# Banded softmax attention in one launch: key low parts and values padded with zeros to 128 rows and 128 columns

## Chip, cores and metric

The kernel runs on one core of a Trainium2 chip. The metric is the device time of one execution in microseconds (us); the lower, the better.

## What is computed

The program is a network of two parts: a first block (a gated delta rule mixer and a convolutional gated feed-forward network) and then two equal layers. The change lies in one of the three mixers of each of these two layers, attention inside a band of 128 positions with a learned bias and a sink. Of 8 query heads, four each share one of two key and value heads (`kv`); a head has 64 features, the sequence 512 positions.

```python
def _window_gqa(q, k, v, rel_bias, sink):
    ...
    kb, vb = band(k), band(v)            # each block of 128 queries sees three blocks of keys
    ...
    s = jnp.einsum('bnqkgd,bnskd->bnkgqs', q, kb).astype(jnp.float32) * (C_DH ** -0.5) + bias
    s = jnp.where(valid[None, :, None, None], s, MASK_VALUE)
    sink_l = sink.astype(jnp.float32).reshape(C_KV_HEADS, G)[:, :, None, None]
    m = jnp.maximum(jnp.max(s, axis=-1, keepdims=True), sink_l)
    p = jnp.exp(s - m)
    p = p / (jnp.sum(p, axis=-1, keepdims=True) + jnp.exp(sink_l - m))
    o = jnp.einsum('bnkgqs,bnskd->bnqkgd', p.astype(v.dtype), vb)
    return o.reshape(Bsz, S, C_HEADS * C_DH)
```

Its result `y_c` goes through a projection, is gated, and is added to those of the two other mixers (`branch` c, a and b in the kernel).

## The kernel before, in words

Activations lie with features on the 128 partitions and the 512 positions along the free dimension. Weights come in tiles of 128 x 1024 by DMA, and each is split into a high part (fp32r, on ScalarE, line 110) and a low part (the rest, on VectorE or GpSimd, line 119). A projection is three products for each tile of 128 x 128 weights and 512 positions: lines 157 (high by high), 158 (high by low) and 159 (low by high). These three lines, "the GEMM products" below, are most of what TensorE does in the whole program.

`window` (lines 883 to 951; stage `win` in names of tiles) does one layer's banded attention. It first makes the keys. For each of the two key heads the 64 feature rows are copied to both halves of a tile `K`, 128 rows, as high parts; one shared tile `Kl` holds the low parts, head 0 in rows 0 to 63, head 1 in rows 64 to 127. Values are transposed into one tile `V`, for each block of 128 keys 64 columns of head 0 and 64 of head 1. Then come four strips `s`; a strip is one projection of two query heads, `h = s` with key head 0 and `h = s + 4` with key head 1. For one head:

- `qq` holds the query's high parts in the rows of its own key head (`R`, 64 rows) and its low parts in the other 64 rows.
- For each of four blocks of 128 queries, line 925 is the score product with `kh` over all 128 rows (high by high and low by high at once), and line 926 adds the high query parts by the low keys: 64 rows of `qq` and of `kl` alone. A block sees 256 or 384 keys.
- Lines 929 to 941 are the softmax on VectorE and ScalarE: bias, row maximum, exponential with its sum, sink, reciprocal, scaling.
- Line 944 transposes the 128 x 128 blocks of probabilities on TensorE, line 946 copies them out of PSUM, and line 948 is the value product: 64 columns of `V` (those of `kv`) give 64 rows `O[R]` of the output. The operands are plain f32, for which the trace shows two weight loads and two matmuls for each product.

After both heads of a strip the 128 x 512 output `O` is copied (line 950) and sent to DRAM (`keep_y`), from where branch c loads it.

Nothing writes out the order of the engines' queues by hand: a scheduler that goes by its own estimates of time lays the instructions of all stages into each engine's queue. In this stage it puts GEMM products of branch a (stage `br`) between the pieces of the window, so TensorE's queue holds window products and GEMM products in turn. An engine takes its queue in that order. The two layers have the same pattern of products in this stage.

In a row of the trace, `128*128` ahead of an operand's shape is the shape of TensorE's array that the instruction uses, rows by columns: 64*128 is half of the rows, 128*64 half of the columns.

Of the kernel before, what the change touches and what calls it, by code (L numbers as in the profile page):

```python
# [9 lines left out]
F32R = mybir.dt.float32r  # L10
# [7 lines left out]
P = 128  # L18
# [5 lines left out]
def f32(ap):  # L24
    return ap.bitcast(F32)
# [590 lines left out]
def window_bias_head(p, h):  # L616

    t = p.t("wb", 3, 384)
    dr = p.relrow[h]
    p.nc.sync.dma_start(t, bass.AP(dr.tensor, dr.offset + 127, [[511, 128], [1, 384]]))  # L620
    return t
# [94 lines left out]
def strip_r(p, name, b, tag="z", bufs=3, pool=None):  # L716

    ps = p.strip(name, b, p.X)
    t = p.t(tag, bufs, keep=tag[0] == "z", pool=pool)
    p.nc.vector.tensor_tensor(t, ps, p.r, MULT)  # L720
    return t
# [9 lines left out]
def keep_y(p, y, ys):  # L731
    d = p.dram([P, 512], "yd")
    p.nc.sync.dma_start(d, y)
    ys.append(d)


def side_by_side(p, ps, out, scale=None):

    nc = p.nc
    v = out.rearrange("p (h k c) -> p h k c", k=2, c=64)  # L740
    hi, lo = v[:, :, 0, :], v[:, :, 1, :]
    src = ps.rearrange("p (h c) -> p h c", c=64)
    if scale is None:
        nc.scalar.activation(hi, src, AF.Copy)
        nc.vector.tensor_tensor(lo, src, f32(hi), SUB)
    else:
        nc.scalar.activation(hi, src, AF.Identity, scale=scale)
        nc.vector.scalar_tensor_tensor(lo, src, scale, f32(hi), MULT, SUB)
    return out
# [4 lines left out]
def mla(p, l, G, low, mid, high):  # L754
# [45 lines left out]
    wvh, wvl = p.wload(f"w_uv{l}", 0, 1024)  # L800
    V = []
    for t in range(4):
        ps = p.ps()
        ts = slice(t * P, t * P + P)
        for k in range(2):
# [4 lines left out]
            nc.tensor.matmul(ps, xl[:, ts], wvh[:, c], start=False, stop=k == 1)  # L810
        V.append(side_by_side(p, ps, p.t("V", 4, 1024, F32R)))

# [14 lines left out]
    for pr in range(4):  # L827
# [6 lines left out]
        for hh in range(2):  # L834
# [10 lines left out]
            Q.append((qh, ql))  # L845
        Y = p.t("x", 3, keep=True)
        for hh in range(2):
            qh, ql = Q[hh]
            for q2 in range(2):
# [21 lines left out]
                for kb in range(4):  # L871
                    v = V[kb][:, (pr * 2 + hh) * P:(pr * 2 + hh) * P + P]
                    nc.tensor.matmul(o, v, pth[:, kb, :], start=kb == 0, stop=False)
                    nc.tensor.matmul(o, v, ptl[:, kb, :], start=False, stop=kb == 3)
                y = Y[half[hh], q2 * 256:q2 * 256 + 256]
                nc.scalar.copy(y, o[64:])
                nc.vector.tensor_tensor(y, o[:64], y, ADD)
        keep_y(p, Y, G.y["a"])

# [3 lines left out]
def window(p, l, G):  # L883
    nc = p.nc
    at = G.at
    w_in = f"w_in{l}"
    half = [slice(0, 64), slice(64, 128)]

    k = strip_r(p, w_in, at["ck"])
    K = []  # L890
    kl = p.t("Kl", 1, dtype=F32R)
    for kv in range(2):
        kh = p.t("K", 2, dtype=F32R)
        for i in range(2):
            nc.scalar.activation(kh[half[i]], k[half[kv]], AF.Copy)
        nc.vector.tensor_tensor(kl[half[kv]], k[half[kv]], f32(kh[half[kv]]), SUB)
        K.append((kh, kl))
    v = strip_r(p, w_in, at["cv"])
    pv = p.ps("b")
    for t in range(4):  # L900
        nc.tensor.transpose(pv[:, t * P:t * P + P], v[:, t * P:t * P + P], p.ident)
    V = p.t("V", 1)
    nc.scalar.copy(V, pv)
    for s in range(4):
        q = strip_r(p, w_in, at["cq2"] + s)
        O = p.ps("o")
        Y = p.t("x", 3, keep=True)
        for kv in range(2):
            h = s + 4 * kv
            R = slice(kv * 64, kv * 64 + 64)  # L910
            qq = p.t("Q", 8, dtype=F32R)
            nc.scalar.activation(qq[R], q[R], AF.Copy)
            nc.gpsimd.tensor_tensor(qq[half[1 - kv]], q[R], f32(qq[R]), SUB)
            kh, kl = K[kv]
            sink = p.col(f"sink{l}")[:, h:h + 1]
            wb = window_bias_head(p, h)
            negm, den, es = (p.small([P, 4], n, 3) for n in ("w4m", "w4d", "w4e"))
            E = []
            for qb in range(4):
                k0, k1 = max(qb - 1, 0), min(qb + 2, 4)  # L920
                W = (k1 - k0) * P
                qs = slice(qb * P, qb * P + P)
                ks = slice(k0 * P, k1 * P)
                sc = p.ps("a")[:, :W]
                nc.tensor.matmul(sc, qq[:, qs], kh[:, ks], start=True, stop=False)
                nc.tensor.matmul(sc, qq[R, qs], kl[R, ks], start=False, stop=True)
                sb = p.t("wsb", 10, 384)[:, :W]
                off = (k0 - qb + 1) * P
                nc.vector.tensor_tensor_reduce(sb, sc, wb[:, off:off + W], 0.125, sink, ADD, MAX,
                                               accum_out=negm[:, qb:qb + 1])  # L930
                nc.vector.tensor_scalar(negm[:, qb:qb + 1], negm[:, qb:qb + 1], -1.0, None, MULT)
                nc.scalar.activation(sb, sb, AF.Exp, bias=negm[:, qb:qb + 1], accum_out=den[:, qb:qb + 1])
                E.append(sb)
            nc.scalar.activation(es, negm, AF.Exp, bias=sink)
            nc.vector.tensor_tensor(den, den, es, ADD)
            nc.vector.reciprocal(den, den)
            for qb in range(4):
                k0, k1 = max(qb - 1, 0), min(qb + 2, 4)
                W = (k1 - k0) * P
                qs = slice(qb * P, qb * P + P)  # L940
                nc.vector.tensor_scalar(E[qb], E[qb], den[:, qb:qb + 1], None, MULT)
                pt = p.ps("b")[:, :W]
                for kb in range(k1 - k0):
                    nc.tensor.transpose(pt[:, kb * P:kb * P + P], E[qb][:, kb * P:kb * P + P], p.ident)
                pts = p.t("pts", 4, 384)[:, :W]
                nc.scalar.copy(pts, pt)
                for kb in range(k0, k1):
                    nc.tensor.matmul(O[R, qs], V[:, kb * P + kv * 64:kb * P + kv * 64 + 64],
                                     pts[:, (kb - k0) * P:(kb - k0) * P + P], start=kb == k0, stop=kb == k1 - 1)
        nc.scalar.copy(Y, O)  # L950
        keep_y(p, Y, G.y["c"])

# [15 lines left out]
def hgrn(p, l, G, pools, tail):  # L968
# [6 lines left out]
    p.rows_gemm(f"w_bi{l}", 0, p.X, pst)  # L975
    V = []
    for t in range(4):
# [170 lines left out]
def branch(p, l, G, pool, n):  # L1148

    nc = p.nc  # L1150
    bi = "abc".index(n)
    Y = [p.split(p.load(d, "yl", 2, pool=pool), "ys", 8, le="g", pool=pool) for d in G.y[n]]
    M = []
# [84 lines left out]
def layer(p, l):  # L1238
# [11 lines left out]
    with p.pool(f"br{l}") as br, p.pool(f"acc{l}") as G.pool:  # L1250
        p.stage = f"br{l}"
        p.WLO_SEQ = "g"
        branch(p, l, G, br, "b")
        p.WLO_SEQ = "v"
        with p.pool(f"win{l}"):
            p.stage = f"win{l}"
            window(p, l, G)
        with p.pool(f"M{l}"):
            p.stage = f"br{l}"
            for n in "ac":  # L1260
                M = branch(p, l, G, br, n)
            p.stage = f"wo{l}"
            out_proj(p, f"w_out{l}", M, p.col(f"g_x{l}"))
# [846 lines left out]
```

## Time and profile before

| | us |
|---|---|
| time, median of 3 runs | 3699.72 |
| the 3 runs | 3694.47 to 3702.97 |
| the profiled execution, its own time | 3706.06 |
| its span, first to last instruction | 3704.2 |
| TensorE busy in the span | 3523.1 (95%) |
| VectorE, ScalarE, GpSimd busy | 2342.8 (63%), 1715.5 (46%), 1190.2 (32%) |
| first score product to last value product, layer 0 | 1688.01 to 1823.66: 135.65 |
| the same, layer 1 | 2959.76 to 3095.41: 135.65 |

"TensorE busy" is the union of the matmuls' spans. These are longer than the distance between their starts, since matmuls overlap; a busy TensorE may still start its products late. The pace of a stretch is therefore read from the starts of its rows in the timeline, not from the busy share.

### The profile page before, as it was taken

Reading aid. Unit: us, or ns where it says so; the run is one execution under the profiler, and the core shown is the slowest. Engines: PE = TensorE matmul, PEld = TensorE weight load, DVE = VectorE, ACT = ScalarE, POOL = GpSimd, SP = SyncE. Lnnn points to the kernel's source line nnn. Section 1 sums busy time; section 2 is a strip of 40 time slices with the busy share of each in tenths; the row PEclk is TensorE's granted clock in tenths of the full one; section 3 lists DMA queues with packets and bytes.
Section 4 is the critical chain, followed back from the end, with each engine's and each line's share of the span. In section 5 each row is a group of like instructions: output and inputs, shape, how many; then the busy total and the mean of one; then the engine's idle time right before and its main releaser. Section 6 shows DMA issues by size and latency. Waiting matters only on the chain.

```text
span 3704.2 us, 51835 instructions
## 1 busy us (share of the span) xinstructions
PE 3523.1 (95%) x19504; PEld 2864.9 (77%) x19504; DVE 2342.8 (63%) x3681; ACT 1715.5 (46%) x3095; POOL 1190.2 (32%) x1109
## 2 busy tenths in 40 slices
PE   7998899989999999899999999998978999999998
PEld 6887788868888787687777888877767877778886
DVE  8878774755543777775556665358768655656643
ACT  3776554344433444565544444244436555444431
POOL 4475774422211333331121221124433312212212
PEclk9999898999999999899999999999989999999999
DMA  4345775533334222222253333421212322432332
GB/s 172 105 109 167 212 235 143 166 123 97 97 108 126 67 71 62 66 87 85 83 159 100 117 97 100 128 86 54 69 46 74 98 74 88 164 109 97 98 102 91
DMA packets 228955, 401.05 MB, mean 108 GB/s; under 512 B 77281, under 2 KB 118497, under 8 KB 228705
## 3 DMA queue, kind: packets, MB, share of 16 engines
q1 hardware_dynamic: 228704, 397.74, 35.0%
q8 instruction: 154, 2.52, 0.3%
q14 instruction: 97, 0.79, 0.1%
HBM read 347.58 MB, written 47.97 MB: 107 GB/s over the span
## 4 chain that ended last, share of the span: by engine, by line
PE 75%; DVE 13%; POOL 3%; issue 3%; ACT 3%; DMA 2%; SPq 0%; DVEq 0%; ACTq 0%; POOLq 0%
PE ffn_psg L158 4%; PE ffn_psg L159 4%; PE ffn_psg L157 4%; PE br_psg L159 4%; PE br_psg L158 3%; PE br_psg L157 3%; PE f_psg L159 2%; PE f_psg L158 2%; PE f_psg L157 2%; PE glu_psg L158 2%; PE glu_psg L159 2%; PE glu_psg L157 2%; PE hg_psg L159 2%; PE hg_psg L157 1%; PE hg_psg L158 1%
## 5 line engine op out<-in xcount | busy, mean ns | idle before, releaser
L159 PE MATMUL ffn_psg<-xo_X,ffn_wl 128*128 128x512 f32 x704 | 274.7, 390 | 0.0
L158 PE MATMUL ffn_psg<-xo_X,ffn_wh 128*128 128x512 f32 x704 | 273.9, 389 | 0.0
L157 PE MATMUL ffn_psg<-xo_X,ffn_wh 128*128 128x512 f32 x704 | 273.9, 389 | 0.0
L119 DVE TENSOR_TENSOR ffn_wl<-ffn_wr,ffn_wh 128x1024 fp32r<-128x1024 f32 x88 | 153.5, 1745 | 19.7 <-ACT ffn_wh L110 19.7
L157 PEld LDWEIGHTS ffn_psg<-xo_X,ffn_wh 128*128 128x128 f32 x704 | 132.1, 188 | 28.1 <-issue 0.5
L159 PEld LDWEIGHTS ffn_psg<-xo_X,ffn_wl 128*128 128x128 f32 x704 | 132.1, 188 | 27.6 <-issue 0.5
L158 PEld LDWEIGHTS ffn_psg<-xo_X,ffn_wh 128*128 128x128 f32 x704 | 132.1, 188 | 27.5
L720 DVE TENSOR_TENSOR ffn_z<-ffn_psg,xo_ry 128x512 f32<-128x512 f32 x88 | 60.7, 692 | 142.8 <-PE ffn_psg L159 142.6
L1232 POOL TENSOR_TENSOR ffn_z<-ffn_z,ffn_z 128x512 f32<-128x512 f32 x44 | 57.3, 1302 | 274.4 <-DVE ffn_z L720 233.8
L159 PE MATMUL f_psg<-ffn_U,f_wl 128*128 128x512 f32 x352 | 140.8, 400 | 0.0
L158 PE MATMUL glu_psg<-gout_X,glu_wh 128*128 128x512 f32 x352 | 137.9, 392 | 3.0 <-DVE gout_X L1368 3.0
L157 PE MATMUL glu_psg<-gout_X,glu_wh 128*128 128x512 f32 x352 | 138.1, 393 | 2.1 <-ACT gout_X L1367 2.1
L119 DVE TENSOR_TENSOR f_wl<-f_wr,f_wh 128x1024 fp32r<-128x1024 f32 (+1 forms) x48 | 56.8, 1183 | 129.6 <-ACT f_wh L110 129.6
L158 PE MATMUL f_psg<-ffn_U,f_wh 128*128 128x512 f32 x352 | 138.7, 394 | 0.0
L157 PE MATMUL f_psg<-ffn_U,f_wh 128*128 128x512 f32 x352 | 138.0, 392 | 0.0
L159 PE MATMUL glu_psg<-gout_X,glu_wl 128*128 128x512 f32 x352 | 137.6, 391 | 0.0
L1164 POOL TENSOR_TENSOR br_acc<-br_acc,br_za 128x512 f32<-128x512 f32 x32 | 44.7, 1398 | 285.7 <-DVE br_za L1163 233.7
L110 ACT ACTIVATE ffn_wh<-ffn_wr 128x1024 fp32r<-128x1024 f32 x88 | 93.7, 1064 | 92.1 <-PE ffn_psg L158 67.5
L110 ACT ACTIVATE f_wh<-f_wr 128x1024 fp32r<-128x1024 f32 (+1 forms) x48 | 47.5, 989 | 167.3 <-PE f_psg L158 134.7
L119 DVE TENSOR_TENSOR glu_wl<-glu_wr,glu_wh 128x1024 fp32r<-128x1024 f32 x44 | 56.4, 1282 | 102.0 <-ACT glu_wh L110 101.8
L110 ACT ACTIVATE br_wh<-br_wr 128x1024 fp32r<-128x1024 f32 x96 | 81.0, 844 | 83.4 <-PE br_psg L158 59.3
L110 ACT ACTIVATE hg_wh<-hg_wr 128x1024 fp32r<-128x1024 f32 x64 | 67.6, 1056 | 108.0 <-PE hg_psg L158 78.3
(853 smaller groups left out, 11558.2 us busy)
## 6 DMA issues: line engine op xcount, KB each, us to landing
ffn_wr<-in_f_w_dram SPq DMA_DIRECT2D x88, 512.0 KB, 3.5
hg_wr<-in_w_in_dram SPq DMA_DIRECT2D x56, 512.0 KB, 3.6
br_wr<-in_w_in_dram SPq DMA_DIRECT2D x48, 512.0 KB, 3.6
glu_wr<-in_ffn_in_dram SPq DMA_DIRECT2D x44, 512.0 KB, 3.5
fill_C<-in_w_mod_dram SPq DMA_DIRECT2D x64, 256.0 KB, 5.4
f_wr<-in_f_w_dram SPq DMA_DIRECT2D x32, 512.0 KB, 3.6
prep_wr<-in_gdn_in_dram SPq DMA_DIRECT2D x24, 512.0 KB, 3.7
fill_wr<-in_x_wk_dram SPq DMA_DIRECT2D x16, 512.0 KB, 4.5
```

Of the source, the lines that this page charges most:

```text
L110: nc.scalar.activation(hi, src, AF.Copy)
L119: e.tensor_tensor(lo, src, f32(hi), ALU.subtract)
L157: nc.tensor.matmul(ps, wh, xh, start=start, stop=False)
L158: nc.tensor.matmul(ps, wh, xl, start=False, stop=False)
L159: nc.tensor.matmul(ps, wl, xh, start=False, stop=stop)
L720: p.nc.vector.tensor_tensor(t, ps, p.r, MULT)
L1164: nc.gpsimd.tensor_tensor(G.acc[m], G.acc[m], a, ADD)
L1232: nc.gpsimd.tensor_tensor(z1, z1, z3, MULT)
```

## The change

- Each key head gets a `Kl` tile of its own, 128 rows, of which the 64 rows of the other head are set to zero on GpSimd. The second score product takes all 128 rows of `qq` and of `kl`. The rows added multiply low query parts by zero.
- Each key head gets a `V` tile of its own, with zeros in the 64 columns of the other head. The one copy out of PSUM becomes two strided copies of 64 columns a block, with one GpSimd memset each.
- A value product takes 128 columns and gives all 128 rows of `O`. The products of both heads add into the same region of PSUM, so one accumulation for each query block holds the key blocks of both heads, and is issued once the second head's probabilities are there (`T` keeps those of the first). `pts` has 8 buffers for that, where it had 4.

The number of score products, transposes and value products is the same as before.

```diff
--- before.py
+++ after.py
@@ -886,25 +886,33 @@
     w_in = f"w_in{l}"
     half = [slice(0, 64), slice(64, 128)]
 
+
     k = strip_r(p, w_in, at["ck"])
     K = []
-    kl = p.t("Kl", 1, dtype=F32R)
     for kv in range(2):
-        kh = p.t("K", 2, dtype=F32R)
+        kh, kl = p.t("K", 2, dtype=F32R), p.t("Kl", 2, dtype=F32R)
         for i in range(2):
             nc.scalar.activation(kh[half[i]], k[half[kv]], AF.Copy)
         nc.vector.tensor_tensor(kl[half[kv]], k[half[kv]], f32(kh[half[kv]]), SUB)
+        nc.gpsimd.memset(f32(kl[half[1 - kv]]), 0.0)
         K.append((kh, kl))
     v = strip_r(p, w_in, at["cv"])
     pv = p.ps("b")
     for t in range(4):
         nc.tensor.transpose(pv[:, t * P:t * P + P], v[:, t * P:t * P + P], p.ident)
-    V = p.t("V", 1)
-    nc.scalar.copy(V, pv)
+
+    V = []
+    for kv in range(2):
+        t = p.t("V", 2)
+        c = lambda a, i: a.rearrange("p (t i c) -> p t i c", t=4, i=2)[:, :, i]
+        nc.scalar.copy(c(t, kv), c(pv, kv))
+        nc.gpsimd.memset(c(t, 1 - kv), 0.0)
+        V.append(t)
     for s in range(4):
         q = strip_r(p, w_in, at["cq2"] + s)
         O = p.ps("o")
         Y = p.t("x", 3, keep=True)
+        T = {}
         for kv in range(2):
             h = s + 4 * kv
             R = slice(kv * 64, kv * 64 + 64)
@@ -923,7 +931,7 @@
                 ks = slice(k0 * P, k1 * P)
                 sc = p.ps("a")[:, :W]
                 nc.tensor.matmul(sc, qq[:, qs], kh[:, ks], start=True, stop=False)
-                nc.tensor.matmul(sc, qq[R, qs], kl[R, ks], start=False, stop=True)
+                nc.tensor.matmul(sc, qq[:, qs], kl[:, ks], start=False, stop=True)
                 sb = p.t("wsb", 10, 384)[:, :W]
                 off = (k0 - qb + 1) * P
                 nc.vector.tensor_tensor_reduce(sb, sc, wb[:, off:off + W], 0.125, sink, ADD, MAX,
@@ -942,11 +950,15 @@
                 pt = p.ps("b")[:, :W]
                 for kb in range(k1 - k0):
                     nc.tensor.transpose(pt[:, kb * P:kb * P + P], E[qb][:, kb * P:kb * P + P], p.ident)
-                pts = p.t("pts", 4, 384)[:, :W]
+                pts = p.t("pts", 8, 384)[:, :W]
                 nc.scalar.copy(pts, pt)
-                for kb in range(k0, k1):
-                    nc.tensor.matmul(O[R, qs], V[:, kb * P + kv * 64:kb * P + kv * 64 + 64],
-                                     pts[:, (kb - k0) * P:(kb - k0) * P + P], start=kb == k0, stop=kb == k1 - 1)
+                T[kv, qb] = pts
+                if kv == 1:
+                    for i in range(2):
+                        for kb in range(k0, k1):
+                            nc.tensor.matmul(O[:, qs], V[i][:, kb * P:kb * P + P],
+                                             T[i, qb][:, (kb - k0) * P:(kb - k0) * P + P],
+                                             start=i == 0 and kb == k0, stop=i == 1 and kb == k1 - 1)
         nc.scalar.copy(Y, O)
         keep_y(p, Y, G.y["c"])
 
```

On TensorE, layer 0, the first value products of strip 0, before (`pts` are the transposed probabilities, `psb` the transposes, `psa` the scores, `psg` a GEMM product):

```order
L157 MATMUL br0_psg_3570_17062<-br0_ys_3559_17013,br0_wh_3572_17065 128x512
L948 MATMUL win0_pso_3357_16276<-win0_pts_3373_16321,win0_V_3351_16241 64x128 x2
L948 MATMUL win0_pso_3357_16276<-win0_pts_3375_16330,win0_V_3351_16241 64x128 x3
L944 MATMUL win0_psb_3376_16336<-cstt_69,win0_wsb_3369_16303 128x128 x3
L944 MATMUL win0_psb_3378_16346<-cstt_69,win0_wsb_3371_16310 128x128 x2
L925 MATMUL win0_psa_3414_16474<-win0_K_3343_16195,win0_Q_3409_16466 128x256
L926 MATMUL win0_psa_3414_16474<-win0_Kl_3342_16194,win0_Q_3409_16466 128x256
L925 MATMUL win0_psa_3416_16481<-win0_K_3343_16195,win0_Q_3409_16466 128x384
L926 MATMUL win0_psa_3416_16481<-win0_Kl_3342_16194,win0_Q_3409_16466 128x384
L158 MATMUL br0_psg_3570_17062<-br0_ys_3560_17014,br0_wh_3572_17065 128x512
```

There a head's value products come ahead of its own later transposes. The same place on TensorE in the changed kernel, whose lines 933, 934, 952 and 959 are the old 925, 926, 944 and 948:

```order
L157 MATMUL br0_psg_3572_17069<-br0_ys_3561_17020,br0_wh_3574_17072 128x512
L952 MATMUL win0_psb_3378_16338<-cstt_69,win0_wsb_3371_16310 128x128 x3
L952 MATMUL win0_psb_3380_16345<-cstt_69,win0_wsb_3373_16317 128x128 x2
L959 MATMUL win0_pso_3359_16283<-win0_pts_3375_16328,win0_V_3352_16244 128x128 x2
L158 MATMUL br0_psg_3572_17069<-br0_ys_3562_17021,br0_wh_3574_17072 128x512
L159 MATMUL br0_psg_3572_17069<-br0_ys_3561_17020,br0_wl_3575_17073 128x512
L157 MATMUL br0_psg_3572_17069<-br0_ys_3564_17026,br0_wh_3574_17072 128x512
L158 MATMUL br0_psg_3572_17069<-br0_ys_3565_17027,br0_wh_3574_17072 128x512
L933 MATMUL win0_psa_3416_16481<-win0_K_3342_16194,win0_Q_3411_16473 128x256
L934 MATMUL win0_psa_3416_16481<-win0_Kl_3343_16195,win0_Q_3411_16473 128x256
L933 MATMUL win0_psa_3418_16488<-win0_K_3342_16194,win0_Q_3411_16473 128x384
L934 MATMUL win0_psa_3418_16488<-win0_Kl_3343_16195,win0_Q_3411_16473 128x384
```

The transposes and the scores of the next head stand where they stood, and of the value products only those of the first block are left here. The others have moved to where the second head's transposes are done; on TensorE, further on in strip 0 of the changed kernel:

```order
L933 MATMUL win0_psa_3437_16546<-win0_K_3344_16200,win0_Q_3432_16538 128x256
L934 MATMUL win0_psa_3437_16546<-win0_Kl_3345_16201,win0_Q_3432_16538 128x256
L959 MATMUL win0_pso_3359_16283<-win0_pts_3396_16393,win0_V_3353_16247 128x128 x2
L959 MATMUL win0_pso_3359_16283<-win0_pts_3377_16335,win0_V_3352_16244 128x128 x3
L959 MATMUL win0_pso_3359_16283<-win0_pts_3398_16404,win0_V_3353_16247 128x128 x3
L952 MATMUL win0_psb_3399_16413<-cstt_69,win0_wsb_3392_16375 128x128 x3
L959 MATMUL win0_pso_3359_16283<-win0_pts_3379_16342,win0_V_3352_16244 128x128 x3
L952 MATMUL win0_psb_3401_16426<-cstt_69,win0_wsb_3394_16382 128x128 x2
L933 MATMUL win0_psa_3439_16553<-win0_K_3344_16200,win0_Q_3432_16538 128x384
L934 MATMUL win0_psa_3439_16553<-win0_Kl_3345_16201,win0_Q_3432_16538 128x384
```

Value products of both heads (`V_3352` and `V_3353`) now alternate on the same output `pso_3359`.

On GpSimd, layer 0, ahead of the window, in the changed kernel (`br_wl` are low parts of the weights of branch b, `br_ys` inputs of branch a, line 921 is the old 913):

```order
L119 TENSOR_TENSOR br_wl_16081<-br_wr_16078,br_wh_16080 128x512
L897 MEMSET win_Kl_16195 64x512
L909 MEMSET win_V_16244 128x4x64
L119 TENSOR_TENSOR br_wl_16102<-br_wr_16099,br_wh_16101 128x1024
L119 TENSOR_TENSOR br_wl_16141<-br_wr_16138,br_wh_16140 128x512
L119 TENSOR_TENSOR br_ys_17009<-br_yl_17006,br_ys_17008 128x512
L119 TENSOR_TENSOR br_ys_17015<-br_yl_17012,br_ys_17014 128x512
L119 TENSOR_TENSOR br_ys_17021<-br_yl_17018,br_ys_17020 128x512
L119 TENSOR_TENSOR br_ys_17027<-br_yl_17024,br_ys_17026 128x512
L897 MEMSET win_Kl_16201 64x512
L909 MEMSET win_V_16247 128x4x64
L921 TENSOR_TENSOR win_Q_16285<-win_z_16281,win_Q_16285 64x512
```

The four memsets of a layer are the only rows that are new in this queue; the others stand in the order of before.

## Rows read from the trace of the kernel before

**Rows 1.** The page: busy time of the engines, share of the span, instructions

```profile
PE 3523.1 (95%) x19504; PEld 2864.9 (77%) x19504; DVE 2342.8 (63%) x3681; ACT 1715.5 (46%) x3095; POOL 1190.2 (32%) x1109
```

**Rows 2.** By stretch: us, busy PE PEld DVE ACT POOL, PEclk, DMA, GB/s

```profile
1840.00:1860.00 20.00, 20.00 (x88) 16.16 (x87) 13.09 (x18) 10.73 (x16) 2.93 (x3) 1.00 0.27 91
1688.01:1823.66 135.65, 135.65 (x656) 100.33 (x655) 69.80 (x197) 69.43 (x158) 24.62 (x17) 1.00 0.25 76
2959.76:3095.41 135.65, 135.65 (x656) 100.33 (x654) 69.79 (x197) 69.45 (x158) 24.63 (x17) 1.00 0.26 76
```

**Rows 3.** TensorE's groups in layer 0's window: count, busy us, mean ns, idle before

```profile
L948 PE MATMUL win_pso<-win_pts,win_V 128*64 128x128 f32 x160 | 22.2, 279 | 0.0
...
L926 PE MATMUL win_psa<-win_Kl,win_Q 64*128 64x384 f32 x16 | 7.0, 438 | 0.0
...
L926 PE MATMUL win_psa<-win_Kl,win_Q 64*128 64x256 f32 x16 | 6.1, 381 | 0.0
```

**Rows 4.** Timeline of TensorE, scores of two blocks: start us, us, line, shapes

```profile
1707.06 0.34 PE L925 MATMUL win_psa<-win_K,win_Q 128*128 128x384 f32 x1
1707.33 0.44 PE L926 MATMUL win_psa<-win_Kl,win_Q 64*128 64x384 f32 x1
1707.69 0.38 PE L925 MATMUL win_psa<-win_K,win_Q 128*128 128x256 f32 x1
1708.01 0.38 PE L926 MATMUL win_psa<-win_Kl,win_Q 64*128 64x256 f32 x1
1708.32 0.50 PE L159 MATMUL br_psg<-gl_X,br_wl 128*128 128x512 f32 x1
1708.66 0.40 PE L157 MATMUL br_psg<-br_ys,br_wh 128*128 128x512 f32 x1
```

**Rows 5.** The same view: value products ahead of transposes, then ahead of GEMM products

```profile
1717.77 0.39 PE L158 MATMUL br_psg<-gl_X,br_wh 128*128 128x512 f32 x1
1718.09 1.31 PE L948 MATMUL win_pso<-win_pts,win_V 128*64 128x128 f32 x10
1719.32 0.77 PE L944 MATMUL win_psb<-cstt,win_wsb 128*128 128x128 f32 x5
1719.84 0.42 PE L925 MATMUL win_psa<-win_K,win_Q 128*128 128x384 f32 x1
1720.19 0.43 PE L926 MATMUL win_psa<-win_Kl,win_Q 64*128 64x384 f32 x1
...
1730.24 0.40 PE L158 MATMUL br_psg<-gl_X,br_wh 128*128 128x512 f32 x1
1730.57 0.87 PE L948 MATMUL win_pso<-win_pts,win_V 128*64 128x128 f32 x6
...
1731.70 0.40 PE L157 MATMUL br_psg<-gl_X,br_wh 128*128 128x512 f32 x1
```

**Rows 6.** The same view: products of other stages that all use 128*128

```profile
1223.52 1.05 PE L1092 MATMUL hg_psa<-hg_hl,hg_ha 128*128 128x128 f32 x8
...
1954.04 0.28 PE L158 MATMUL cr_psa<-cr_K,cr_Q 128*128 128x256 f32 x1
...
1954.52 0.28 PE L157 MATMUL cr_psa<-cr_K,cr_Q 128*128 128x256 f32 x1
```

**Rows 7.** VectorE's timeline: scaling of one head's probabilities, the last step of its softmax

```profile
1714.43 1.28 DVE L941 TENSOR_SCALAR win_wsb<-win_wsb,win_w4d 128x256 f32<-128x256 f32 x4
```

**Rows 8.** GpSimd's timeline ahead of the window of layer 0

```profile
1653.23 4.43 POOL L119 TENSOR_TENSOR br_wl<-br_wr,br_wh 128x1024 fp32r<-128x1024 f32 x2 [5.49 <-ACT br_wh L110]
...
1682.60 2.66 POOL L913 TENSOR_TENSOR win_Q<-win_z,win_Q 64x512 fp32r<-64x512 f32 x2 [10.12 <-ACT win_Q L912]
```

**Rows 9.** A group of GpSimd's memsets: count, busy us, mean ns, idle before

```profile
L963 POOL MEMSET hg_hmb<- 128x512 f32 x4 | 2.1, 530 | 10.8 <-PE f_psg L158 10.8
```

**Rows 10.** Weight loads of value products and of transposes: ns min/median/max

```profile
L944 PEld LDWEIGHTS win_psb<-cstt,win_wsb x160: 137/140/143, 1704.2 to 3088.4; 128*128 128x128 f32 x160
...
L948 PEld LDWEIGHTS win_pso<-win_pts,win_V x320: 132/137/137, 1710.4 to 3095.1; 128*64 128x64 f32 x160
```

## The prediction

> **What bounds the kernel now.** I read the page first: TensorE is the busiest engine, 95% of the span [rows 1]. That share can't say whether the two window stages, which are all that the change touches, hang on TensorE, so the stretches come next. From the first score product to the last value product each layer takes 135.65 us; TensorE is busy for all of it, at a granted clock of 1.00, the 2.4 GHz level, while VectorE and ScalarE have 70 us of work there, GpSimd 25, and DMA is at a quarter [rows 2]. So nothing but TensorE's own queue sets the length of this stage: what is taken from TensorE there comes off the end, until another engine is late.
>
> But busy is not at its peak, and the last view, the timeline of starts, shows what the stage loses. In branch c without a window, 88 products of 512 columns take 20.00 us, 0.227 each [rows 2]. In the window a score product over 256 or 384 columns, which should be shorter than that, has 0.31 to 0.37 us to itself: starts at 1707.33, 1707.69, 1708.01 and 1708.32 [rows 4]. Each of these steps goes from an instruction of the shape 128*128 to one of 64*128 or back. Products of 256 columns that all have the shape 128*128 start every (1954.52 - 1954.04) / 4 = 0.12 us in another stage [rows 6]. The value products show the same: within a run of 128*64 they start every (0.87 - 0.28) / 5 = 0.118 to (1.31 - 0.28) / 9 = 0.114 us, but 0.32 or 0.33 us pass from the GEMM product ahead of the run to its first, and 0.33 us for the GEMM product behind [rows 5] (0.28 is the mean length of one [rows 3]; runs overlap, so the distance of starts is what counts).
>
> **The change part by part.**
>
> *Low key products at 128 rows.* In [rows 4] two blocks and the GEMM product behind them take 1708.66 - 1707.06 = 1.60 us. With one shape throughout, a product of 256 columns takes 0.12 [rows 6] and the GEMM product 0.227 [rows 2]. For 384 columns at 128*128 in a stream no row is to be had; it lies between the prices of 256 and of 512 columns, and I take the middle, 0.173. The new sum is 2 x 0.173 + 2 x 0.12 + 0.227 = 0.81, so two blocks save 0.79 us. A layer has 16 low products of 384 and 16 of 256 columns [rows 3], so 16 such pairs of blocks: 12.6 us. With 0.12 for 384 columns it would be 14.3, with 0.227 10.9. The rows added to the product cost nothing by themselves: the price goes by columns streamed, as both score products of a block show by having about the same length of step at 128 and at 64 rows [rows 4].
>
> *Value products at 128 columns.* 160 instructions a layer [rows 3], as many as before; the timeline of the window has them in 22 runs. At 128*128 the nearest row for a plain f32 product with 128 columns of weights and 128 streamed is a run of 8 in 1.05 us: (1.05 - 0.28) / 7 = 0.11 [rows 6]; I take 0.11. A run that ends in GEMM products (4 of the 22): 1731.70 - 1730.24 = 1.46 us for two GEMM products and 6 value products, against 2 x 0.227 + 6 x 0.11 = 1.11; saved 0.35. One that ends in transposes (18 of 22): 1719.84 - 1717.77 = 2.07 us for a GEMM product, 10 value products and 5 transposes, against 0.227 + 15 x 0.11 = 1.88; and the score product behind starts early but then takes 0.35 in place of the 0.27 of [rows 4], so 0.08 of the transposes is hidden in it; saved 0.19 + 0.08 = 0.27. Sum 4 x 0.35 + 18 x 0.27 = 6.3 us a layer.
>
> The wider weights are the place where a rule speaks against the change. The load of 64 columns takes 137 ns in this trace and that of 128 columns 140 [rows 10], so here the width hardly shows. The Trainium skill (TensorE: Matmul & The Clock Gate, section "LDWEIGHTS (loading the stationary operand)") has the load's time go with the number of columns, P / 1.2 ns, 53 against 107: as an estimate by that page, 320 loads would bring 17 us back if none were hidden, and the saving would be 21. By the rows none of it shows.
>
> *The order.* The first head's value products now wait in TensorE's queue for the second head's probabilities, and behind a value product that waits stand GEMM products and the next scores; the copy of O (line 950), its DMA and branch c wait for the last of them. The order shown above puts them behind the second head's transposes with other products between. Nothing of this waits by itself; whether the softmax is in time there is the first rival. Ends: 0 and, with 1 us at every fourth of the 16 heads (two layers), 4 us. I take 0: in [rows 4, 5, 7] a head whose last score starts at 1708.01 has its probabilities scaled by 1714.43 + 1.28 = 1715.71, and its transposes run at 1719.32 without a wait, 3.6 us in hand.
>
> *Zeros and copies.* Four memsets a layer of at most 128 x 256 or 64 x 512, where one of 128 x 512 took 0.53 us [rows 9]: at most 2.1 us a layer on GpSimd, in front of low parts of weights of branch b and of the queries. GpSimd has been idle for 5.5 us ahead of the first and 10.1 us ahead of the second place [rows 8], so they are hidden; with that cover gone it is 4 us in all. One more copy of V on ScalarE, half empty in this stage [rows 2], is hidden in the same way. Six GEMM products stand elsewhere in the second layer's start; 6 x 0.227 is 1.4 us either way.
>
> **Sum.** 12.6 + 6.3 = 18.9 us a layer, 37.8 for two. Against the profiled execution 3706.06 - 37.8 = 3668.3; it was 6.3 us above the median of the runs, 3699.72, and against that the sum is **3662**. As a check from the other side, the 655 products of a layer's window at pure prices are 351 GEMM products x 0.227 + 32 score products x 0.12 + 32 x 0.173 + 240 f32 products x 0.11 = 115.4 us of the 135.65; that leaves 20.2 a layer if no step loses anything, 40.5 in all. What is late next is TensorE again: the stage would have 70 us of VectorE in 117, and branch c alone feeds 88 products in 20 us with a DMA share of 0.27 [rows 2], faster than the window will ask.
>
> **The rivals.**
>
> *The softmax becomes late.* With fewer microseconds in the same products, the cover between a head's last score and its transposes shrinks. At the tightest place of the new order (second head of strip 0) 19 + 6 GEMM products, 5 transposes, 4 value instructions and 6 score products stand between: 25 x 0.227 + 9 x 0.11 + 2 x 0.12 + 4 x 0.173 = 7.6 us. The chain in [rows 4, 7] takes 7.7 us to the last of four scalings, 6.8 to the first. So waits of some tenths are likely at one or two heads of a layer. A wait of 1 us at each of the 16 heads would make it 3678. It turns *slower than before* where the chain exceeds its cover by 37.8 / 16 = 2.4 us at every head; at 3 us, 48 - 37.8 gives 3710. Against it: VectorE and ScalarE are at half load [rows 2], and the chain's own pieces are short.
>
> *Weights of 128 columns are not hidden.* If a value product went at the load's 0.14 us [rows 10] plus the 0.05 by which the first of a run is late, 0.19 in place of 0.11, 320 instructions would give 25.6 us back: 3688. Against it stand the transposes and the run in [rows 6], both 128 columns wide at 0.11. The Trainium skill's rule on the load by columns is cited above.
>
> *The loss is not due to the shape.* The steps of [rows 4] also change the operand from `kh` to `kl`. Were that the cause, the scores would keep their pace and 12.6 x 2 = 25 us would stay: 3687; were it so for the value products too, 3700. Against it: in [rows 6] high and low operands alternate at 0.12. The Trainium skill (TensorEngine Tiling (Array Packing), section "Key Properties") says that a change of the tiling mode drains TensorE; by that rule the loss goes with the shapes, and the trace agrees, 0.37 against 0.12.
>
> **How the numbers follow.** Forecast as summed, 3653 to 3675: 0.78. Softmax late, 3675 to 3690: 0.12. Weights not hidden: 0.03. Loss not of the shape: 0.03, half of it within 0.2%. Slower by the softmax: 0.04. The lower end takes in the pure prices (40.5), 384 columns at 0.12 (3.4 more) and the runs' own spread, 5 us below their median: 3652. The upper end takes 384 columns at 0.227 (3.4 less), waits of 4, memsets of 4 and GEMM products of 1.4, which gives 3675, and part of the first rival: 3681. A difference of 0.2%, about 7 us, is what a measurement of this kernel can tell from none. Faster by more than that 0.92, within it 0.03, slower 0.05.
>
> **What would show it.** Right: both windows at 115 to 119 us with TensorE busy throughout; no row with 64*128 or 128*64 left in them; low score products 0.12 and 0.17 behind the high ones; value products at 0.11 with no step of 0.2 or 0.3 at a run's ends; the rest of the span as before. Wrong: idle time of TensorE ahead of transposes, ended by VectorE or ScalarE (first rival); value products at 0.14 or more (second); low score products still 0.3 or more (third); or a window that is 19 us shorter and a later stage that is longer by as much.

## The result

| | before | changed | ratio, 95% interval |
|---|---|---|---|
| first comparison, median us | 3697.09 | 3653.63 | 0.989, 0.987 to 0.9909 |
| second (`e1_again`) | 3690.56 | 3664.56 | 0.9923, 0.9898 to 0.9947 |
| third (`e6_beside`) | 3690.75 | 3661.88 | 0.9913, 0.9887 to 0.9939 |

The changed kernel is faster by about 1%. The sum of the prediction, 37.8 us, is a ratio of 0.9898; it lies in all three intervals, at the end of the second, and 3653.63 lies in the predicted range of 3652 to 3681.

The page of the profile after, the answer to [rows 1]:

```profile
PE 3467.7 (95%) x19504; PEld 2852.9 (78%) x19504; DVE 2346.7 (64%) x3681; ACT 1712.1 (47%) x3097; POOL 1195.6 (33%) x1117
```

TensorE has the same 19504 instructions and 55 us less of busy time. Where it went is read stretch by stretch. The stretch that holds the whole of the change runs from the first product of the window stage to the last of the branch stage behind it, since it contains the same 1030 TensorE products in every kernel here that adds none. Columns as in [rows 2]. Before, first layer and second:

```profile
1663.92:1885.54 221.62, 221.47 (x1030) 170.05 (x1029) 121.96 (x262) 112.76 (x220) 43.44 (x31) 1.00 0.28 89
2935.67:3157.28 221.61, 221.46 (x1030) 170.05 (x1029) 121.89 (x261) 112.79 (x220) 43.43 (x31) 1.00 0.29 88
```

After, the same two stretches, and below them the first layer's window alone, from the first score product to the last value product, the answer to [rows 2] (the second's is as long):

```profile
1650.12:1853.06 202.94, 202.72 (x1030) 171.26 (x1029) 126.03 (x262) 111.12 (x221) 43.58 (x33) 1.00 0.32 97
2902.90:3106.26 203.36, 202.73 (x1030) 171.25 (x1029) 125.91 (x261) 111.21 (x221) 43.57 (x33) 1.00 0.33 96
1674.20:1785.98 111.78, 111.78 (x634) 97.41 (x633) 71.97 (x196) 65.74 (x155) 20.94 (x15) 1.00 0.28 84
```

The two stretches are 18.68 and 18.25 us shorter, 36.9 together. The window alone seems to save 24 us, but it now holds 634 products where it held 656 (a row also counts products that lie on its edges): 23 GEMM products have moved behind it and are done in the branch. This is why the stretch must hold the same work on both sides. These windows go to the end of the last product; to its start, as some expectations below count, it is 111.5.

The profiled span fell by 50.8 us, 14 more than the two stretches give. Those 14 arise ahead of the first window, where TensorE's queue is the same in both kernels. Here is the part from the inversion stage to the end of the scan, in the profile of before, in the first of the changed kernel and in its third, `e6_beside`:

```profile
235.00:745.00 510.00, 471.04 (x3776) 400.78 (x3775) 363.19 (x741) 263.06 (x637) 302.87 (x402) 0.91 0.61 179
```

```profile
232.00:729.00 497.00, 456.19 (x3764) 387.90 (x3765) 360.99 (x745) 262.72 (x637) 303.92 (x402) 0.94 0.63 183
```

```profile
235.00:747.00 512.00, 473.23 (x3767) 402.51 (x3765) 354.81 (x740) 262.91 (x636) 304.12 (x402) 0.90 0.60 178
```

The changed kernel shows both lengths, 497 us at a mean granted clock of 0.94 and 512 at 0.90; the profile of before happens to be of the long kind. Nor does the length go with the kernel: the first product of the window stage starts at 1663.92 us before, and in the experiments below at 1663.87 (`e2_keys`), 1665.15 (`e8_turns`) and 1666.04 (`e6_beside`), but between 1644.88 and 1650.37 in the first profile of the changed kernel, `e3_values`, `e4_order`, `e5_lowx3` and `e9_strip`. So these 14 us are no effect of the change. They are also why whole times resolve no more than about 0.25% here, and why the experiments are read in the stretches. TensorE's busy time in a stretch of the changed kernel repeats to 0.03 us from profile to profile, its length to 0.2 us in the first layer and 1.4 us in the second.

TensorE's groups in the first layer's window, the answer to [rows 3] (count, busy us, mean ns, idle before):

```profile
L959 PE MATMUL win_pso<-win_pts,win_V 128*128 128x128 f32 x160 | 20.4, 275 | 0.0
...
L934 PE MATMUL win_psa<-win_Kl,win_Q 128*128 128x384 f32 x16 | 5.4, 337 | 0.0
```

The 64*128 and 128*64 rows are gone. What the pace is, only starts tell. The timeline of TensorE, scores of two blocks and the GEMM products behind them, then a run of value products ahead of transposes, the answers to [rows 4] and [rows 5]:

```profile
1695.28 0.28 PE L933 MATMUL win_psa<-win_K,win_Q 128*128 128x256 f32 x1
1695.40 0.28 PE L934 MATMUL win_psa<-win_Kl,win_Q 128*128 128x256 f32 x1
1695.52 0.34 PE L933 MATMUL win_psa<-win_K,win_Q 128*128 128x384 f32 x1
1695.69 0.34 PE L934 MATMUL win_psa<-win_Kl,win_Q 128*128 128x384 f32 x1
1695.87 0.39 PE L159 MATMUL br_psg<-br_ys,br_wl 128*128 128x512 f32 x1
1696.10 0.39 PE L157 MATMUL br_psg<-gl_X,br_wh 128*128 128x512 f32 x1
...
1705.80 1.95 PE L959 MATMUL win_pso<-win_pts,win_V 128*128 128x128 f32 x16
1707.58 0.49 PE L952 MATMUL win_psb<-cstt,win_wsb 128*128 128x128 f32 x3
1707.91 0.83 PE L959 MATMUL win_pso<-win_pts,win_V 128*128 128x128 f32 x6
```

Two blocks and the GEMM product behind them take 1696.10 - 1695.28 = 0.82 us, where they took 1.60. The 16 value instructions take 1707.58 - 1705.80 = 1.78, 0.111 each, and neither their first nor the transpose behind them starts late.

### The profile page after: what moved, and what is told of

The parts are those of the page before. It is cut to its first block, busy times and chain, and to the rows that moved or that the text cites. A ratio compares the mean times of both kernels' runs of the same rounds, so it can differ in the third digit from the quotient of the medians.

```text
span 3653.4 us, 51836 instructions
## 1 busy us (share of the span) xinstructions
PE 3467.7 (95%) x19504; PEld 2852.9 (78%) x19504; DVE 2346.7 (64%) x3681; ACT 1712.1 (47%) x3097; POOL 1195.6 (33%) x1117
## 4 chain that ended last, share of the span: by engine, by line
PE 73%; DVE 12%; POOL 5%; ACT 3%; issue 3%; DMA 2%; SPq 0%; DVEq 0%; ACTq 0%; POOLq 0%
PE ffn_psg L157 4%; PE ffn_psg L159 4%; PE ffn_psg L158 4%; PE br_psg L159 3%; PE br_psg L157 3%; PE br_psg L158 3%; PE f_psg L159 2%; PE f_psg L158 2%; PE f_psg L157 2%; PE glu_psg L158 2%; PE glu_psg L159 2%; PE glu_psg L157 2%; PE hg_psg L159 2%; PE hg_psg L157 1%; PE hg_psg L158 1%
```

## The experiments

All of them are read in the stretch of 1030 products, first layer and second, unless the text says otherwise.

**One part at a time.** `e2_keys` is the kernel before with the key part alone:

```diff
-                nc.tensor.matmul(sc, qq[R, qs], kl[R, ks], start=False, stop=True)
+                nc.tensor.matmul(sc, qq[:, qs], kl[:, ks], start=False, stop=True)
```

and the zeroed `Kl` tiles that this needs. 

> The key part alone: low key products at 128 rows, zeros in Kl; values and their order as in the kernel before. Theory (each change of the array's shape costs time): both score products at 128*128, 384 columns at 0.177 and 256 at 0.119 us, two blocks save 0.79 us, 16 pairs a layer: 25 us below the kernel before (22 to 27), windows about 12.5 us shorter. Rival (the step belongs to the change of operand from high to low keys, or to the row ahead): 0. Rival (the gain of the whole change came from the values and their order): 0 to 5 below.

```profile
1663.87:1872.81 208.94, 208.79 (x1030) 168.47 (x1029) 120.23 (x262) 112.58 (x220) 43.89 (x32) 1.00 0.31 95
```

12.68 us less, and 12.65 in the second layer (208.96), 25.3 together; whole time 3667.03, ratio 0.9935 (0.9913 to 0.9957). The operands still change from high to low keys, so that rival falls.

`e3_values` is the changed kernel with the key part undone. 

> The value part alone: V padded, value products at 128*128, both heads behind the second one's transposes; low key products at 64 rows as in the kernel before. Theory (change of shape): 44 runs of value products in the two layers lose 0.27 to 0.35 us each no more: 12.6 us below the kernel before (10 to 14), and the two parts add up to the whole change. Rival (the wider weights cost something that the scores hid): 5 or less. Rival (softmax late without the key part): 0 or slower.

```profile
1644.88:1860.13 215.25, 215.19 (x1030) 172.69 (x1029) 126.70 (x262) 111.36 (x221) 43.46 (x32) 1.00 0.30 92
2909.47:3125.16 215.69, 215.17 (x1030) 172.64 (x1029) 126.59 (x261) 111.44 (x221) 43.44 (x32) 1.00 0.29 91
```

6.37 and 5.92 us less, 12.3 together, as the theory had it. The whole time, 3681.74, ratio 0.9974 (0.9956 to 0.9992), stands for anything from 3 to 16 us less and does not tell the theory from its first rival; the stretches do. The two parts give 37.6 us, the whole change 36.9: they add up.

**Is a product on 64 rows slow, or the change of shape?** `e5_lowx3` issues each low product of the kernel before three times:

```diff
-                nc.tensor.matmul(sc, qq[R, qs], kl[R, ks], start=False, stop=True)
+                for i in range(3):
+                    nc.tensor.matmul(sc, qq[R, qs], kl[R, ks], start=False, stop=i == 2)
```

> The kernel before with each low key product issued three times into the same sum (the scores are not the reference's): 64 extra products of 64*128 a layer that follow one of their own shape. Theory (the time goes with the change of shape, a product of 64 rows is as quick as one of 128): each extra product takes 0.119 us at 256 columns and 0.177 at 384, so 9.5 us a layer, first score to last value product from 135.65 to about 145. Rival (a product on 64 rows is slow by itself, 0.31 and 0.36): 21 us a layer, about 157.

 The scheduler also placed fewer GEMM products inside the window, so 135.65 against 130.7 compares unlike work; the timeline of TensorE and the stretch, with 64 products more, do not have this fault:

```profile
1674.24 0.28 PE L925 MATMUL win_psa<-win_K,win_Q 128*128 128x256 f32 x1
1674.45 0.61 PE L927 MATMUL win_psa<-win_Kl,win_Q 64*128 64x256 f32 x3
1674.99 0.44 PE L925 MATMUL win_psa<-win_K,win_Q 128*128 128x384 f32 x1
1675.36 0.80 PE L927 MATMUL win_psa<-win_Kl,win_Q 64*128 64x384 f32 x3
1676.09 0.50 PE L159 MATMUL win_psg<-gl_X,win_wl 128*128 128x512 f32 x1
```

```profile
1650.15:1881.38 231.23, 230.35 (x1094) 178.93 (x1093) 129.94 (x262) 112.45 (x220) 42.94 (x31) 1.00 0.28 86
2931.40:3166.02 234.62, 232.13 (x1094) 180.06 (x1093) 130.04 (x261) 112.15 (x220) 43.91 (x31) 0.99 0.28 83
```

Three low products of 256 columns take 1674.99 - 1674.45 = 0.54 us, where one took 0.31 or 0.32 [rows 4]: 0.115 for each extra one. With 384 columns it is 0.73, where one took 0.36: 0.185. The first layer's stretch is 9.6 us longer, as the theory had it. A product on 64 rows behind one of its own shape is as quick here as one on 128 rows; what costs is the step from one shape to the other and back. The second layer's stretch, at 234.62 against 221.61, is 13.0 us longer; it had 2.5 us of waiting and a mean granted clock of 0.99, the only one here apart from that of `e9_strip` below 1.00.

**The order alone.** `e4_order` has the changed kernel's order of value products and the 8 buffers of `pts`, with 64 columns of an unpadded `V` as before:

```diff
-                for kb in range(k0, k1):
-                    nc.tensor.matmul(O[R, qs], V[:, kb * P + kv * 64:kb * P + kv * 64 + 64],
+                T[kv, qb] = pts
+                if kv == 1:
+                    for i in range(2):
+                        for kb in range(k0, k1):
+                            nc.tensor.matmul(O[half[i], qs], V[:, kb * P + i * 64:kb * P + i * 64 + 64],
```

> The order of the value part alone: both heads' value products behind the second head's transposes, pts with 8 buffers, but V as before and products at 128*64. TensorE's queue then has 32 runs of value products in the two layers, as the changed kernel has, where the kernel before has 44. Theory (each run costs two changes of shape, about 0.3 us): 12 runs fewer save 3.6 us (2 to 5), the other 9 us of the value part come with the shape. Rival (the value part gains by its order): 12 us below. Rival (waiting for the second head costs): at or above the kernel before, with TensorE idle ahead of line 952 or so.

```profile
1646.66:1863.09 216.43, 215.17 (x1030) 166.66 (x1029) 124.46 (x262) 111.85 (x220) 42.35 (x31) 1.00 0.30 91
2911.68:3127.80 216.12, 215.19 (x1030) 166.65 (x1029) 124.24 (x261) 112.03 (x220) 42.32 (x31) 1.00 0.30 90
```

My theory missed: 5.19 and 5.49 us less, 10.7 together, near the number of the rival, and TensorE's busy time is that of `e3_values` to 0.02 us; so is the whole time, with 3682.98 and a ratio of 0.9973 (0.9954 to 0.9991). The timeline of TensorE shows a mechanism that neither had:

```profile
1707.60 1.31 PE L952 MATMUL win_pso<-win_pts,win_V 128*64 128x128 f32 x16
1708.83 0.55 PE L945 MATMUL win_psb<-cstt,win_wsb 128*128 128x128 f32 x3
1709.31 0.87 PE L952 MATMUL win_pso<-win_pts,win_V 128*64 128x128 f32 x6
1710.11 0.44 PE L945 MATMUL win_psb<-cstt,win_wsb 128*128 128x128 f32 x2
```

16 value instructions take 1708.83 - 1707.60 = 1.23 us from their first to the transpose behind. In [rows 5] ten took as long, 1719.32 - 1718.09, and in the changed kernel 16 take 1.78. The run of 16 holds products of both heads, for the two halves of the columns and of `O`; the run of 6 holds one head's only and takes 0.80, or 0.13 each. So two column halves of the array work side by side as soon as both have work in one run, which the order before, one head at a time, never gave them. The Trainium skill (TensorEngine Tiling (Array Packing), section "Key Properties") says that different tiles of a mode load and multiply in parallel, and the trace agrees.

**Heads that take turns.** `e8_turns` uses that: the changed kernel's keys and order, `V` unpadded, and 64-column products of the two heads in turn.

```diff
-                    for i in range(2):
-                        for kb in range(k0, k1):
-                            nc.tensor.matmul(O[:, qs], V[i][:, kb * P:kb * P + P],
+                    for kb in range(k0, k1):
+                        for i in (1, 0):
+                            nc.tensor.matmul(O[half[i], qs], V[:, kb * P + i * 64:kb * P + i * 64 + 64],
```

> The changed kernel's keys (low products at 128 rows) and its order, but values unpadded, and within a block of queries the heads take turns: 64-column products into rows 64 to 127 and rows 0 to 63 of O one behind the other. In the run with the new order and 64 columns such products of the two heads started in pairs, 0.109 us a pair. Theory (two column halves work side by side): 160 instructions take 80 x 0.109 = 8.7 us a layer in place of 160 x 0.112 = 17.9; 14 runs a layer at 0.29 for entering and leaving the shape give 4.1 back; about 5 us a layer and 10 in all below the changed kernel. Rival (pairs cost as much as two products once every product has its partner ahead): 8 us above the changed kernel.

```profile
1726.85 1.31 PE L953 MATMUL win_pso<-win_pts,win_V 128*64 128x128 f32 x20
1728.10 0.55 PE L946 MATMUL win_psb<-cstt,win_wsb 128*128 128x128 f32 x3
```

```profile
1665.15:1864.36 199.21, 197.93 (x1030) 160.24 (x1029) 124.14 (x262) 110.64 (x220) 42.93 (x32) 1.00 0.33 99
2913.02:3113.47 200.45, 197.91 (x1030) 160.28 (x1029) 125.07 (x261) 110.73 (x220) 43.36 (x32) 1.00 0.33 97
1689.23:1795.92 106.69, 106.69 (x634) 86.29 (x632) 69.00 (x195) 64.97 (x155) 19.58 (x14) 1.00 0.30 87
```

Twenty instructions take 1.25 us from their first to the transpose behind, ten pairs in the time that ten single ones took in [rows 5], and the window with the same 634 products is 111.78 - 106.69 = 5.1 us shorter than the changed kernel's. TensorE's busy time in the stretch falls by 4.8. Against the changed kernel on the same chip (`e6_beside`, just below) the two stretches are 3.85 and 4.35 us shorter, 8.2 in all where 10 were expected: the busy time gives 9.6 of them, and TensorE waits 1.3 and 2.5 us where it waited 0.3 and 2.1. Its median is 3652.83 against 3661.88, the ratio to before 0.9887 (0.9863 to 0.9911); the intervals of the two overlap, so for the whole time the gain over the changed kernel is likely and not proven.

**The changed kernel beside it.** 

> The changed kernel beside the two variants that take turns, so that they are compared on one chip: 0.985 to 0.992 of the kernel before, window to window as in its first profile (111.5 us from first score to last value product).

```profile
1666.04:1869.10 203.06, 202.74 (x1030) 171.39 (x1029) 126.11 (x262) 110.99 (x221) 43.54 (x33) 1.00 0.32 97
2913.84:3118.64 204.80, 202.74 (x1030) 171.39 (x1029) 125.89 (x261) 111.17 (x221) 43.52 (x33) 1.00 0.32 95
```

Ratio 0.9913. Busy times and the windows are as in the first profile, but the second layer's stretch has 2.1 us of waiting. The second comparison was `e1_again`. 

> The changed kernel once more, beside the kernel before on the same chip. Two windows with their branches are 36.8 us shorter in its first profile (18.6 and 18.2), the profiled span 50.8 us. Theory (the change acts in the two windows alone, and the 14 us left are a difference of the scan stage from one execution to another): the time is 36 to 38 us below the kernel before, and in a profile the stages ahead of the first window move by several us either way. Rival (the first 740 us are shorter with the change too): 43 to 50 us below.

 Its ratio is worth 28 us, with an interval of 20 to 38: the theory's 36 to 38 is at its edge, the rival's 43 to 50 outside. In its profile the two stretches are 203.09 and 204.60 us long, 18.5 and 17.0 less than before. With the third profile, whose part ahead of the windows is long (512 us, above), the rival falls.

**All value products of a strip together.** `e9_strip` moves the loop of `e8_turns` behind the transposes of all four blocks. 

> As the run with heads taking turns, but the value products of a strip are issued behind the transposes of all four blocks, so that fewer runs remain (11 a layer). Theory: 9.2 us less for the pairs, 11 x 0.29 = 3.2 back: 6 us a layer and 12 in all below the changed kernel. Rival (the copy of O and branch c now wait): the gain is seen in the window and lost behind it.

```profile
1650.37:1849.03 198.66, 197.55 (x1030) 161.16 (x1029) 127.39 (x262) 110.39 (x220) 43.06 (x32) 1.00 0.32 100
2901.66:3104.66 203.00, 200.15 (x1030) 163.11 (x1029) 126.06 (x261) 110.18 (x220) 43.94 (x32) 0.98 0.32 96
```

The theory missed: against the changed kernel (`e6_beside`) the stretches are 4.4 and 1.8 us shorter. It went the rival's way in the second layer: there the stretch is 2.6 us longer than that of `e8_turns`. Only 0.3 us of this are more waiting, 2.85 against 2.54; the other 2.2 are TensorE's busy time, 200.15 against 197.91, at a mean granted clock of 0.98. The longest waits, 1.1 and 1.6 us within 5 us, are for inputs of branch c that GpSimd makes; behind them the granted clock falls to 0.50, the 1.2 GHz level, for some 4 us, and GEMM products start 0.43 us apart. The row of waits in the stretch, and two of these 4 us:

```profile
PE br_psg L158 <- POOL br_ys L119: 2.7, 2, 1.6
...
3044.00:3046.00 2.00, 2.00 (x5) 1.58 (x6) 1.00 (x3) 1.15 (x2) 0.00 (x0) 0.50 0.30 114
```

The median was 3658.04, ratio 0.9906 (0.9884 to 0.9927): no gain on `e8_turns` is shown.

**Was the softmax nearly late?** `e7_late1` and `e7_late3` are the changed kernel with one and with three more passes over each head's probabilities ahead of the reciprocal:

```diff
+            for i in range(3):
+                for x in E:
+                    nc.vector.tensor_scalar(x, x, 1.0, None, MULT)
             nc.vector.reciprocal(den, den)
```

> The changed kernel with one more pass of VectorE over the probabilities (times 1.0) ahead of the reciprocal, in each head: the chain from the last score to the scaled probabilities is about 1.3 us longer. In the changed kernel's trace the first transposes of a head start about 3.1 us behind the scaling that they need. Theory (the softmax has some 3 us in hand): no wait of TensorE, window unchanged at 111.5 us. Rival (cover of 7.6 against a chain of 7.7 us, as the prediction had it at the tightest place): a wait of about 1.3 us at each of 16 heads, 10 us a layer.

 

> The same with three more passes: the chain is about 4 us longer than in the changed kernel. Theory (3.1 us in hand): where the order of the queue is as before, about 0.9 us of waiting at each of 8 heads of a layer, 5 to 8 us a layer; where the scheduler has moved the transposes back by its own estimate, less. Rival (no cover): 4 us at each head, 30 us a layer.

 The first layer's window with three passes (with one it is 111.70 us long):

```profile
1670.35:1781.99 111.64, 111.64 (x634) 97.36 (x633) 97.31 (x292) 65.40 (x155) 22.00 (x15) 1.00 0.28 84
```

No wait in either, though VectorE is busy for 97 of 112 us here. So both rivals fall, but how much the softmax has in hand is not shown. With one pass the chain did not grow by 1.3 us where it is tightest: the first transposes of the first two heads start 3.0 and 3.2 us behind the last scaling, in the changed kernel 3.3 and 3.2. With three passes the scheduler put several groups of transposes of the first strips some GEMM products further back, so that case shows that there was work to put in between and not that the old order had 4 us in hand. Each was run once, with 3660.31 and 3657.13 us.

## Why the prediction was right

**TensorE's queue sets the stage, and the loss is in steps between shapes.** Right. Each of the three marks it named is there: no row of the half shapes, low products 0.12 and 0.17 behind the high ones, no late step at the ends of a run. `e2_keys` and `e5_lowx3` rule out the operand and the 64 rows themselves. The Trainium skill's rule on a change of mode, cited in the prediction, is in line with this; the size is this case's own: two blocks with a GEMM product took 1.60 us [rows 4] and now take 0.82, so each of their four steps from shape to shape cost about 0.2 us. (The prediction's 0.37 against 0.12 compares 384 columns with 256; by [rows 4] and the rows after it is 0.36 against 0.17 or 0.18 for 384, and 0.31 against 0.12 for 256.) The windows themselves, at 111.8 us, lie below the 115 to 119 foreseen, since the prediction did not reckon with GEMM products moving out of them; with these 23, 23 x 0.23 = 5.3 us, a window would be 117 us long.

**Low key products, 12.6 us a layer.** Measured 12.7. The price that had no row, 384 columns at 0.173, came out at 0.17 to 0.18.

**Value products, 6.3 us a layer.** TensorE's busy time fell by 221.47 - 215.19 = 6.3 in `e3_values`, the stretches by 6.4 and 5.9. The price of 0.11 was 0.111, so the weights' 128 columns cost nothing that shows, and the second rival falls.

**The order, 0.** Right for this change as far as the sum shows (padded values in the old order were not run), incomplete in its reason. I had weighed the order only for waits. `e4_order` shows that with 64 columns it would have brought 10.7 of the 12.3 us by itself: fewer runs, and column halves that work side by side. With 128 columns there is no second half to work, but also no loss at the ends of the 16 runs that are left in a layer; on TensorE's busy time the two come out even. So the padding of the values was not needed for the gain that the value part made, while the sum for the padded form was sound.

**Zeros and copies, hidden.** Right. GpSimd in the changed kernel's first layer:

```profile
1634.00 0.52 POOL L897 MEMSET win_Kl<- 64x512 f32 x1
1634.58 0.31 POOL L909 MEMSET win_V<- 128x256 f32 x1
1639.43 4.42 POOL L119 TENSOR_TENSOR br_wl<-br_wr,br_wh 128x1024 fp32r<-128x1024 f32 x2 [4.54 <-ACT br_wh L110]
...
```

With the second key head's pair, as long and some 25 us later, that is 1.65 us a layer, under the bound of 2.1, and GpSimd then idles for another 4.5 us.

**The softmax as first rival.** It had 0.12 and did not come. The waits of some tenths that the prediction thought likely are in no row, since the cover worked out for the tightest place, 7.6 against a chain of 7.7 us, was wrong. The second head of strip 0 in the changed kernel, its last score, its scaling and its first transposes:

```profile
1691.37 0.28 PE L934 MATMUL win_psa<-win_Kl,win_Q 128*128 128x256 f32 x1
1696.80 1.26 DVE L949 TENSOR_SCALAR win_wsb<-win_wsb,win_w4d 128x256 f32<-128x256 f32 x4
1701.28 0.71 PE L952 MATMUL win_psb<-cstt,win_wsb 128*128 128x128 f32 x5
```

The cover is 1701.28 - 1691.37 = 9.9 us, with 33 GEMM products in it and not 25, and the chain takes 6.7 us to the last scaling.

**What is late next.** Here the prediction was wrong in a small term. It named TensorE again and argued from branch c's DMA share. In fact TensorE now waits, in branch c, for the window's own last output, which goes to DRAM and back. The timeline of `e6_beside`, second layer:

```profile
3050.34 0.33 SPq L733 DMA_DIRECT2D win_yd<-win_x  x1
...
3056.35 0.33 SPq L98 DMA_DIRECT2D br_yl<-win_yd  x1
3059.06 0.63 ACT L110 ACTIVATE br_ys<-br_yl 128x512 fp32r<-128x512 f32 x1 [3.03 <-DMA br_yl<-win_yd]
...
3059.74 0.50 PE L157 MATMUL br_psg<-br_ys,br_wh 128*128 128x512 f32 x1 [2.00 <-ACT br_ys L110]
```

Before, the write landed after 2.0 us there, and now after 4.5, 5.8 and 5.9 us in the three profiles (DMA issues, before and `e6_beside`):

```profile
win_yd<-win_x SPq DMA_DIRECT2D x1, 256.0 KB, 2.0
```

```profile
win_yd<-win_x SPq DMA_DIRECT2D x1, 256.0 KB, 5.9
```

TensorE's wait for it is 0.6 to 2.0 us in the second layer and up to 0.3 in the first, and 2.3 and 1.0 in `e8_turns`, which gives part of its gain back by it. In `e9_strip` the write lands after 2.0 us, but two loads of branch c take 4.7 and 4.9. Why the write takes longer was not tried. One thing beside it has changed: in `e6_beside` three loads were issued in the 2.3 us ahead of it, and the last of them landed at 3054.32, 4 us behind the start of the write; before, the last load had landed 2.6 us ahead of it. That the write shares the DMA with these loads is likely and not shown.

**The number.** 3662 was made against the median of three runs; the first comparison gave 3653.63, the other two 3664.56 and 3661.88. As differences from the kernel before that is 43.5, 26.0 and 28.9 us, against 37.8. The stretches say 36.9, 35.5 and 35.4 us in three profiles, and TensorE's busy time in them 37.5: the sum was right to 0.3 us for the products, and up to 2.1 us of waiting, which it put at nothing, came back. What the medians differ by beyond that is not in the two stretches. The profiles put it ahead of the first window, most of it in the scan stage; for the medians that is inferred. So it is likely chance that the first comparison came out 8 us below the forecast, close to the lower end of the range. That end is itself off by 1: 40.5, 3.4 and 5 us from 3699.72 leave 3651, not 3652.

## What to carry to other kernels

Look at TensorE's starts, not at its busy share: where small products of another array shape stand between full ones, each step from shape to shape cost about 0.2 us here, more than a small product itself (0.11 to 0.18). Two ways out were measured: pad to the full shape with zeros, which cost nothing that shows here, or give both column halves of the array work in the same run, which did two products in the time of one. And compare stretches that hold the same work on both sides; a scheduler moves other work across any nearer boundary.

## What the runs showed of the hardware

Products of 128*64 on the two column halves overlap whether the heads take turns or come one behind the other (`e8_turns`, `e4_order`): 20 instructions in 1.25 us, 16 in 1.23, against 0.111 each at the full shape. Entering and leaving that shape costs about 0.3 us a run, an estimate from `e8_turns`: its pairs alone would save 160 x 0.111 - 80 x 0.109 = 9.0 us a layer, the busy time fell by 4.8, and 14 runs took the rest. A change from one column half to the other costs nothing that these times show. The granted clock in the scan differs from one execution of the same kernel to the next (0.94 and 0.90), and that part is 497 and 512 us long.
